# Shifting SBUF tiles to multiples of 256 bytes in a two-block transformer kernel

## The chip, the cores and the metric

The kernel runs on one core of one Trainium2 chip. The metric is the device time of one execution in microseconds (us), the median of several. Nothing is shared with another core.

## The reference: what is computed

Two blocks of two layers each, batch 1, in float32, width 1024. The first block works on 512 latent and 256 context tokens, the second on the 512 latent tokens alone.

```python
# first block, per layer: modulated norm, mixer, residual, squared-relu MLP (hidden width 4096)
x = x + mod_l[:, :, 2] * y_l
x = x + mod_l[:, :, 5] * sq_relu_mlp(modulate(x, norm2_g[layer], mod_l, 3), mlp_w1[layer], mlp_w2[layer])
# layer 0 mixes by an mLSTM and window attention, layer 1 by attention over context and latents
# second block, per layer (hidden width 2816)
def swiglu_half(x, w1, w3, w2):
    return 0.5 * ((jax.nn.silu(x @ w1) * (x @ w3)) @ w2)
x = layer_norm(ALPHA * x + swiglu_half(x, ffn1...), ...)
mix = concatenate([spatial_gating(...), gated_deltanet(...), gla(...)]) @ w_out[l]
x = layer_norm(ALPHA * x + mix, ...)
x = layer_norm(ALPHA * x + swiglu_half(x, ffn2...), ...)
```

## The kernel before

Almost all of the work is dense products of 128x128 blocks. To keep float32 accuracy each factor is split into a high part H and a low part L, both of the type float32r, and `mm3` (L154) issues three matmuls into the same PSUM bank: high by high, high by low, low by high. In a matmul one operand stands in the array (a weight load, 128 columns, ahead of each matmul) and the other moves through it (mostly 512 columns). In the trace a row such as `ps<-hH,wh` names the moving operand first and the standing one second.

Weights arrive by DMA in `wf` (two buffers of 8 KB per partition), ScalarE copies them to `wh`, VectorE takes the difference to `wl` (four buffers of 4 KB each). These three pools are opened first on the right side of SBUF (L205), where addresses are handed out downward from the upper end. All other right-side pools (the residual tiles `xl`, `tm`, the attention keys `kv0`, the tiles of the second block's mixers) lie below them.

On the left side, handed out upward, lie in this order: `const` (identity, masks, `mod`), then `hT`, the transposed activations of the latents, `hH` and `hL` (L216, 128 x 8 x 512 each); then, in the first block, the small tiles `sm1`, then `hTc`, the transposed context activations `hcH` and `hcL` (L326), then the tiles of the stage at hand: the inner features `hid` of the squared-relu MLP (L1156), the rows, keys, values and probabilities of layer 1 (`rows1`, `rows1b`). In the second block there are `sm2` and then, in each gated feed-forward, the pool `hidf` with scratch `sl` (three buffers), the inner features `hidH` and `hidL` (13 buffers each) and behind it the pool `wx` with four more weight buffers.

The dense products have four shapes:

- feature-major (`genA`, and the first products of the MLPs and feed-forwards): a 128-column block of `wh` or `wl` stands, `hH` or `hL` moves with 512 columns (`hcH`, `hcL` with 256).
- second product of the squared-relu MLP (`genP` with `lhs` from `hid`): a block of `hid` stands, `wh` or `wl` moves.
- token-major products of the mixers and of the attention layer (`genP`, `genB`): a block of `hH`, `hL` or `hcH`, `hcL` stands, `wh` or `wl` moves.
- second product of the gated feed-forward (`gen2`): a block of `hidH` or `hidL` stands, `wh` or `wl` moves.

The gate of the gated feed-forward is `glu` (L1833 and on): ScalarE writes Silu of the first product to `sl`, VectorE multiplies it with the second product and 0.5, then ScalarE copies it to `hidH` and VectorE writes the rest to `hidL`. The order of all instructions is fixed when the program is built; a rough clock of the builder weaves the chains of the mixers between the dense products, but no tile's address enters into it.

Of the kernel before, what the change touches and what calls it, by code (L numbers as in the profile page):

```python
# [25 lines left out]
# order of emission in the mixers: priorities of chains, backlog they may see, order of the projections  # L26
# [8 lines left out]
N6, NQ, N5, N5B = 9, 4, 13, 15  # L35

# [11 lines left out]
class Lane:  # L48
    """an engine whose calls are passed on and added to a rough clock, for the order of emission"""
# [53 lines left out]
class Slots:  # L103
    """tiles handed out and given back in the order of emission"""
# [11 lines left out]
class Net:  # L116
# [73 lines left out]
    def right(self, es, name, bufs=1):  # L190
        return es.enter_context(self.tc.tile_pool(name=name, bufs=bufs, side="right", reuse_waits="tile"))

    def pool(self, es, name, **kw):
        return es.enter_context(self.tc.tile_pool(name=name, bufs=1, side="left", reuse_waits="tile", **kw))

# [1 line left out]
    def run(self):  # L197
        with ExitStack() as es:
            self.es = es
            tc, nc, I = self.tc, self.nc, self.I  # L200
            self.flip = False
            cp = self.pool(es, "const")
            self.cp = cp
            self.psp = es.enter_context(tc.tile_pool(name="psum", bufs=8, space=PSUM))
            self.wf, self.wh, self.wl = self.right(es, "wf", 2), self.right(es, "wh", 4), self.right(es, "wl", 4)  # L205
            self.dp = es.enter_context(tc.tile_pool(name="scratch", bufs=1, space=bass.MemoryType.DRAM))
            cm = cp.tile([128, 8, 128], F32, name="cmat")
            nc.sync.dma_start(cm, I["cmat"])
            self.ident, self.U, self.Ub, self.maskF, self.maskB, self.U64, self.S64 = [cm[:, i, :] for i in range(7)]
            self.I64 = cm[:, 7, 0:64]  # L210
            self.ones = cp.tile([128, 128], F32, name="ones")
            nc.vector.memset(self.ones, 1.0)
            self.mhalf = cp.tile([128, 16], F32, name="mhalf")
            nc.vector.memset(self.mhalf, -0.5)
            hp = self.pool(es, "hT")
            self.hT = hp.tile([128, 8, 512], F32R, name="hH"), hp.tile([128, 8, 512], F32R, name="hL")  # L216
            if self.start == "all":
                self.first_specs()
            if self.stop not in ("L0mix", "L0", "L1"):
                self.second_specs()  # L220
            if self.start == "all":
                self.first_block()
            if self.stop not in ("L0mix", "L0", "L1"):
                self.second_block()
            else:
                self.xes.close()
# [10 lines left out]
    # ================= first block =================  # L237
# [3 lines left out]
    def tok(self, t):  # L241
        """features by tokens of tile t: context 0, 1, latents 2..5"""
        a, i = (self.hTc, t) if t < 2 else (self.hT, t - 2)
        c = slice(i * 128, i * 128 + 128)
        return a[0][:, :, c], a[1][:, :, c]
# [12 lines left out]
    def mild(self, i):  # L258
        """pieces whose low parts GpSimd takes: all of them, or the second half of each"""
        n = len(self.specs)  # L260
        if i in SLOW0:
            self.slow |= {n, n + 1}
        if -i - 1 in SLOW0:
            self.slow |= {-n, -n - 1}
# [45 lines left out]
    # feature blocks of layer 0's projection: columns, width, pieces of modulation weights between  # L310
# [34 lines left out]
    def ada_setup(self):  # L345
        nc, I, cp = self.nc, self.I, self.cp
        self.mark("ada")
        cc = self.sm.tile([16, 128], F32, tag="cc", name="cc", bufs=1)
        nc.sync.dma_start(cc[0:8, :], I["c"][0].rearrange("(k p) -> k p", p=128))
        nc.sync.dma_start(cc[8:16, :], I["c_ctx"].rearrange("(k p) -> k p", p=128))  # L350
        gr = self.sm.tile([32, 128], F32, tag="gr", name="gr", bufs=1)
        for i, n in enumerate(("norm1_g", "norm2_g")):
            nc.sync.dma_start(gr[16 * i:16 * i + 16, :], I[n].rearrange("l (k p) -> (l k) p", p=128))
        self.act(cc, cc, AF.Silu)
        p = self.pb.get()
        nc.tensor.transpose(p[:, 0:16], cc, self.ident[0:16, 0:16])
        nc.tensor.transpose(p[:, 16:48], gr, self.ident[0:32, 0:32])
        self.sT = self.sm.tile([128, 8, 32], F32, tag="sT", name="sT", bufs=1)
        nc.vector.memset(self.sT, 0.0)
        nc.vector.tensor_copy(self.sT[:, :, 0:1], p[:, 0:8].unsqueeze(2))  # L360
        nc.vector.tensor_copy(self.sT[:, :, 1:2], p[:, 8:16].unsqueeze(2))
        self.gF = self.sm.tile([128, 2, 2, 8], F32, tag="gF", name="gF", bufs=1)
        nc.vector.tensor_copy(self.gF.rearrange("p a b c -> p (a b c)"), p[:, 16:48])
        self.pb.put(p)
        # [layer, latents or context, part of the modulation, feature block]
        self.mod = cp.tile([128, 2, 2, 6, 8], F32, name="mod")
        self.mD = [[self.dp.tile([128, 512], F32, name=f"mD{l}{s}") for s in range(3)] for l in range(2)]
# [18 lines left out]
    def ada_first(self, c, n, f):  # L386
        """half c of shift and scale of the first norm, two row blocks"""
        r = 64 * c
        if n == 0:
            self.abanks[c] = self.pb.get()  # L390
        for k in range(2):
            for s in range(2):
                self.nc.tensor.matmul(self.abanks[c][r + 32 * s:r + 32 * s + 32, :], lhsT=self.sT[:, 2 * n + k, :], rhs=f[:, k, s, :],
                                      start=n + k == 0, stop=n == 3 and k == 1)
                self.pe(0.43)
        if n == 3:
            self.spawn(self.ch_first(c), 0)
# [44 lines left out]
    def gate_row(self, pool, l, i, r):  # L442
        """row of modulation i (2 or 5) for all partitions"""
# [7 lines left out]
    def ch_mod(self, t, x, l, i, name, tm, keep=True):  # L451
        """modulated rms norm of token tile t, by features and split; x as two halves of 512"""
# [44 lines left out]
    def genP(self, tiles, width, evac, raw=(), lhs=None, gate=None):  # L497
        """token-major product with eight row blocks of weights, token tiles by pairs"""
# [32 lines left out]
    def layer0(self):  # L531
# [9 lines left out]
        # keys of a head above themselves, and their low parts  # L541
# [11 lines left out]
        # norm of the inputs while the modulation is on its way  # L553
# [88 lines left out]
        # -- window attention  # L642
# [171 lines left out]
        def ch_switch():  # L814
            """room for the rest once the window attention is done"""
# [6 lines left out]
        # -- mLSTM  # L822
# [313 lines left out]
    def gated(self, x, p, g):  # L1136
        """x += g * p"""
# [97 lines left out]
    def layer1(self):  # L1235
# [121 lines left out]
        def ch_rl(g, t, rl):  # L1357
            """rows of the reciprocal sums, for all partitions"""
# [157 lines left out]
    def specraw(self, q):  # L1516
        """pieces of the modulation weights, used as they are"""
# [12 lines left out]
    def issue(self):  # L1530
        """loads for which a buffer is free"""
# [12 lines left out]
    def wsplit(self):  # L1544
        """closures that split the next piece"""
# [45 lines left out]
    def ahead(self):  # L1591
        """queue the split of the next weights"""
# [20 lines left out]
    def specA(self, w, c0, n, extra=False):  # L1613
        """columns c0..c0+n of w, output features by 128"""
# [9 lines left out]
    def genA(self, n, evac, more=(), take=tuple):  # L1624
        """n pieces of up to two output tiles of 128 features, 512 tokens; evac gives the bank back"""
# [12 lines left out]
    def genB(self, toks, width, evac):  # L1638
        """token-major, token tiles by pairs; evac gives the bank back"""
# [19 lines left out]
    # ================= second block =================  # L1659
# [81 lines left out]
    def g_layer_norm(self, y, n, eps, g, b):  # L1741
        """in place (y - mean) * rsqrt(var + eps) * g + b over n columns"""
# [15 lines left out]
    def chain_T(self, t, x):  # L1758
        """x transposed and split into the columns of tile t of hT"""
# [37 lines left out]
    def gen2(self, hs, epi):  # L1797
        """token-major product of the hidden tiles with 1024 columns"""
# [24 lines left out]
    def ffn(self, l, p, ln, dump):  # L1823
# [3 lines left out]
        with ExitStack() as es:  # L1827
# [5 lines left out]
            def glu(p1, p3, hs):  # L1833
                s_ = hid.tile([128, 512], F32, tag="sl", name="sl", bufs=3)
# [63 lines left out]
    def mixers(self, l):  # L1898
# [13 lines left out]
        # conv weights by feature, spatial biases by token  # L1912
# [54 lines left out]
        # small constants of the layer  # L1967
# [22 lines left out]
        def ch_gdn_gates():  # L1990
# [31 lines left out]
            # row of the cumulated gates of the chunk for its tokens  # L2022
# [118 lines left out]
        def ch_inv():  # L2141
# [20 lines left out]
            # E for the queries: keys up to the query of the same chunk  # L2162
# [19 lines left out]
        def head_out(out, ov, gate, nh, sq_, p, ev):  # L2182
            """rms norm per head of 64 of ov (PSUM), times gate"""
# [154 lines left out]
        def ch_prep():  # L2338
            """inverses and off-diagonal blocks of a tile as diagonal blocks"""
# [354 lines left out]
```

## Time and profile before

| | |
|---|---|
| median of 3 runs | 3851.73 us (3850.28 to 3855.07) |
| span of the profiled execution | 3851.4 us |
| TensorE matmuls busy | 3754.8 us, 97% of the span |
| weight loads busy | 3016.6 us, 78% |
| VectorE, ScalarE, GpSimd busy | 1893.6, 1316.6, 324.7 us |
| DMA | 379.65 MB, mean 99 GB/s |
| mean granted TensorE clock | 0.990 of full speed |

The profiled execution's span is 0.3 us below the median of the runs. In the chain of work that ended last TensorE holds 86%, VectorE 7%, ScalarE 2%, DMA 1%.

The matmuls of one TensorE queue overlap: the profile shows each from its start to its modelled end, and the next one starts before that. The pace of a stretch is read from the starts: the first and the last row of a timeline, divided by the number of matmuls between.

### The profile page before, as it was taken

Reading aid. Unit: us, or ns where it says so; the run is one execution under the profiler, and the core shown is the slowest. Engines: PE = TensorE matmul, PEld = TensorE weight load, DVE = VectorE, ACT = ScalarE, POOL = GpSimd, SP = SyncE. Lnnn points to the kernel's source line nnn. Section 1 sums busy time; section 2 is a strip of 40 time slices with the busy share of each in tenths; the row PEclk is TensorE's granted clock in tenths of the full one; section 3 lists DMA queues with packets and bytes.
Section 4 is the critical chain, followed back from the end, with each engine's and each line's share of the span. In section 5 each row is a group of like instructions: output and inputs, shape, how many; then the busy total and the mean of one; then the engine's idle time right before and its main releaser. Section 6 shows DMA issues by size and latency. Waiting matters only on the chain.

```text
span 3851.4 us, 46517 instructions
## 1 busy us (share of the span) xinstructions
PE 3754.8 (97%) x18941; PEld 3016.6 (78%) x18941; DVE 1893.6 (49%) x3367; ACT 1316.6 (34%) x2213; POOL 324.7 (8%) x283
## 2 busy tenths in 40 slices
PE   8999899999999999999999999999999999999998
PEld 5676777777877778878888878888888888778887
DVE  4646663333368654443334586433433355864334
ACT  4547441211345532232222543222222225423221
POOL 1202200000011000000000241000000002410000
PEclk9999999999999999999999999999999999999999
DMA  6214542433221122223323421232333234212222
GB/s 241 69 50 143 170 167 99 156 99 102 66 72 57 42 91 88 91 96 99 104 83 121 103 80 66 89 103 82 99 99 104 89 116 102 77 66 93 99 88 82
DMA packets 282310, 379.65 MB, mean 99 GB/s; under 512 B 49224, under 2 KB 207296, under 8 KB 276976
## 3 DMA queue, kind: packets, MB, share of 16 engines
q1 hardware_dynamic: 282096, 376.68, 30.4%
q8 instruction: 148, 2.42, 0.3%
q14 instruction: 66, 0.54, 0.0%
HBM read 359.50 MB, written 17.15 MB: 98 GB/s over the span
## 4 chain that ended last, share of the span: by engine, by line
PE 86%; DVE 7%; ACT 2%; POOL 1%; DMA 1%; issue 1%; SPq 0%; POOLq 0%; ACTq 0%; DVEq 0%
PE ps L142 82%; PE ps L151 3%; POOL r L81 1%; PE ps L380 1%; DVE wl L81 1%; DVE x L81 1%; DVE ui L81 1%; DVE ua L81 1%; DVE hL L81 1%; DVE mx L81 0%; DMA fa<-in_ada_w_dram 0%; DVE st L81 0%; ACT wh L81 0%; DVE tm L81 0%; DVE u L81 0%
## 5 line engine op out<-in xcount | busy, mean ns | idle before, releaser
L81 ACT ACTIVATE wh<-wf 128x1024 fp32r<-128x1024 f32 (+2 forms) x516 | 538.0, 1050 | 1493.7 <-PE ps L142 1261.4
L81 DVE TENSOR_TENSOR wl<-wf,wh 128x1024 fp32r<-128x1024 f32 (+2 forms) x496 | 600.3, 1216 | 809.2 <-ACT wh L81 808.8
L142 PE MATMUL ps<-hH,wh 128*128 128x512 f32 (+1 forms) x2336 | 885.6, 380 | 6.8 <-ACT hH L81 5.6
L142 PE MATMUL ps<-hL,wh 128*128 128x512 f32 (+1 forms) x2336 | 881.8, 378 | 0.0
L142 PE MATMUL ps<-hH,wl 128*128 128x512 f32 (+1 forms) x2336 | 881.0, 377 | 0.0
L142 PEld LDWEIGHTS ps<-hH,wh 128*128 128x128 f32 x2336 | 440.0, 189 | 108.0 <-issue 9.5
L142 PEld LDWEIGHTS ps<-hL,wh 128*128 128x128 f32 x2336 | 440.8, 189 | 88.8 <-DVE ss L81 1.7
L142 PEld LDWEIGHTS ps<-hH,wl 128*128 128x128 f32 x2336 | 440.7, 189 | 88.3
L142 PE MATMUL ps<-wh,hid 128*128 128x512 f32 x1280 | 405.1, 395 | 0.0
L81 POOL TENSOR_TENSOR r<-rs,mhalf 128x1 f32<-128x1 f32 (+4 forms) x112 | 135.9, 1215 | 2775.4 <-DVE rs L81 2760.7
L142 PE MATMUL ps<-wh,hH 128*128 128x512 f32 (+3 forms) x800 | 315.3, 395 | 3.8 <-ACT uc L81 2.1
L142 PE MATMUL ps<-wh,hL 128*128 128x512 f32 (+3 forms) x800 | 303.4, 380 | 4.5 <-DVE hL L81 4.2
L142 PE MATMUL ps<-wl,hH 128*128 128x512 f32 (+3 forms) x800 | 302.3, 379 | 1.0 <-DVE wl L81 1.0
L142 PEld LDWEIGHTS ps<-wh,hid 128*128 128x128 f32 x1280 | 239.6, 187 | 58.0
L142 PE MATMUL ps<-wh,hidH 128*128 128x512 f32 x704 | 274.3, 390 | 0.0
L142 PE MATMUL ps<-wl,hidH 128*128 128x512 f32 x704 | 274.0, 389 | 0.0
L142 PE MATMUL ps<-wh,hidL 128*128 128x512 f32 x704 | 273.9, 389 | 0.0
L142 PE MATMUL ps<-wl,hid 128*128 128x512 f32 x640 | 252.5, 394 | 0.0
L81 DVE SCALAR_TENSOR_TENSOR sl<-sl,ps 128x512 f32<-128x512 f32 x88 | 60.5, 687 | 259.7 <-PE ps L142 259.6
L142 PEld LDWEIGHTS ps<-wh,hH 128*128 128x128 f32 x800 | 152.1, 190 | 43.3 <-issue 5.8
L142 PEld LDWEIGHTS ps<-wh,hL 128*128 128x128 f32 x800 | 152.3, 190 | 36.9 <-DVE hL L81 7.4
L142 PEld LDWEIGHTS ps<-wl,hH 128*128 128x128 f32 x800 | 152.7, 191 | 26.2 <-DVE wl L81 1.5
(369 smaller groups left out, 4740.7 us busy)
## 6 DMA issues: line engine op xcount, KB each, us to landing
wf<-in_ffn_w_dram SPq DMA_DIRECT2D x120, 1024.0 KB
wf<-in_mlp_w_dram SPq DMA_DIRECT2D x64, 1024.0 KB
wf<-in_ada_w_dram SPq DMA_DIRECT2D x40, 1024.0 KB
wf<-in_w_in_dram SPq DMA_DIRECT2D x24, 1024.0 KB
wf<-in_ffn_w_dram SPq DMA_DIRECT2D x24, 512.0 KB
wf<-in_ab_w_in_dram SPq DMA_DIRECT2D x10, 1024.0 KB
fa<-in_ada_w_dram SPq DMA_DIRECT2D x16, 512.0 KB
wf<-in_w_out_dram SPq DMA_DIRECT2D x16, 512.0 KB
```

The costliest lines, as they stand in the source:

```text
L81: r = f(*a, **kw)
L142: self.nc.tensor.matmul(out, lhsT=l, rhs=r, start=start, stop=stop)
L151: self.nc.tensor.transpose(out, in_, self.ident)
L380: self.nc.tensor.matmul(self.abank[32 * j:32 * j + 32, :], lhsT=self.sT[:, k, :], rhs=f[:, 512 * j:512 * j + 512], start=k == 0, stop=k == 7)
```

## The change

Every pool whose name is in a new table gets one more tile, allocated first and never used, so that all later tiles of that side move by its size. A pool `edge` is opened ahead of the weight buffers on the right side. The scratch `sl` of the gated feed-forward has two buffers in place of three. Nothing else changes but comments, which are taken out: the instructions, their order and their operands' sizes are the same.

```diff
+PAD = {'const': 64, 'sm1': 160, 'hidf': 224, 'edge': 224}
...
     def right(self, es, name, bufs=1):
-        return es.enter_context(self.tc.tile_pool(name=name, bufs=bufs, side="right", reuse_waits="tile"))
+        p = es.enter_context(self.tc.tile_pool(name=name, bufs=bufs, side="right", reuse_waits="tile"))
+        if name in PAD:
+            p.tile([128, PAD[name] // 4], F32, name="pad" + name, bufs=1)
+        return p
 
     def pool(self, es, name, **kw):
-        return es.enter_context(self.tc.tile_pool(name=name, bufs=1, side="left", reuse_waits="tile", **kw))
+        p = es.enter_context(self.tc.tile_pool(name=name, bufs=1, side="left", reuse_waits="tile", **kw))
+        if name in PAD:
+            p.tile([128, PAD[name] // 4], F32, name="pad" + name)
+        return p
...
+            self.right(es, "edge")
             self.wf, self.wh, self.wl = self.right(es, "wf", 2), self.right(es, "wh", 4), self.right(es, "wl", 4)
...
-                s_ = hid.tile([128, 512], F32, tag="sl", name="sl", bufs=3)
+                s_ = hid.tile([128, 512], F32, tag="sl", name="sl", bufs=2)
```

## Rows read from the trace of the kernel before

**Rows 1.** Page, head and section 1: span, and busy time of each engine.

```profile
span 3851.4 us, 46517 instructions
PE 3754.8 (97%) x18941; PEld 3016.6 (78%) x18941; DVE 1893.6 (49%) x3367; ACT 1316.6 (34%) x2213; POOL 324.7 (8%) x283
```

**Rows 2.** Busy time by stretch: length, engines, granted clock, DMA share, GB/s.

```profile
60.00:541.00 481.00, 453.06 (x2305) 338.09 (x2303) 284.20 (x784) 249.92 (x601) 97.05 (x80) 0.98 0.38 126
541.00:1106.00 565.00, 565.00 (x2902) 453.21 (x2903) 229.21 (x352) 145.86 (x228) 3.75 (x7) 1.00 0.30 100
1106.00:1358.00 252.00, 238.12 (x1156) 190.39 (x1154) 189.32 (x489) 128.66 (x291) 25.54 (x30) 0.98 0.18 57
1734.00:2110.00 376.00, 375.67 (x1754) 311.08 (x1753) 137.32 (x158) 97.32 (x120) 6.05 (x4) 1.00 0.31 99
2110.00:2418.00 308.00, 298.84 (x1919) 242.08 (x1919) 215.54 (x400) 132.25 (x204) 81.02 (x63) 0.98 0.29 85
```

**Rows 3.** Groups by form, TensorE: moving, standing operand, shape, count, busy, mean ns.

```profile
L142 PE MATMUL ps<-hH,wh 128*128 128x512 f32 x1952 | 776.7, 398 | 0.0
L142 PE MATMUL ps<-wh,hid 128*128 128x512 f32 x1280 | 405.1, 395 | 0.0
L142 PE MATMUL ps<-wh,hidH 128*128 128x512 f32 x704 | 274.3, 390 | 0.0
L142 PE MATMUL ps<-wl,hH 128*128 128x512 f32 x640 | 256.1, 401 | 0.0
L142 PE MATMUL ps<-wl,hcH 128*128 128x512 f32 x128 | 52.5, 410 | 0.0
L142 PE MATMUL ps<-hH,wl 128*128 128x256 f32 x384 | 108.5, 284 | 0.0
L142 PE MATMUL ps<-hcH,wl 128*128 128x256 f32 x256 | 71.3, 278 | 0.0
```

**Rows 4.** Timeline of TensorE, feed-forward, feature-major: start, length; 104 rows.

```profile
1925.84 0.40 PE L142 MATMUL ps<-hL,wh 128*128 128x512 f32 x1
...
1949.87 0.40 PE L142 MATMUL ps<-hH,wl 128*128 128x512 f32 x1
```

**Rows 5.** Timeline, squared-relu MLP, second product: 105 matmuls.

```profile
629.62 0.63 PE L142 MATMUL ps<-wh,hid 128*128 128x512 f32 x2
...
653.89 0.39 PE L142 MATMUL ps<-wl,hid 128*128 128x512 f32 x1
```

**Rows 6.** Timeline, output projection of a mixer, token-major: 69 matmuls.

```profile
2395.95 0.39 PE L142 MATMUL ps<-wh,hH 128*128 128x512 f32 x1
...
2411.81 0.40 PE L142 MATMUL ps<-wh,hL 128*128 128x512 f32 x1
```

**Rows 7.** Timeline, gated feed-forward, second product: 107 matmuls.

```profile
1867.79 0.39 PE L142 MATMUL ps<-wl,hidH 128*128 128x512 f32 x1
...
1891.82 0.39 PE L142 MATMUL ps<-wh,hidL 128*128 128x512 f32 x1
```

**Rows 8.** Timeline, context half of the MLP: two groups of 24.

```profile
565.80 0.28 PE L142 MATMUL ps<-hcH,wh 128*128 128x256 f32 x1
...
568.63 0.39 PE L142 MATMUL ps<-hH,wh 128*128 128x512 f32 x1
...
573.52 0.28 PE L142 MATMUL ps<-hcH,wh 128*128 128x256 f32 x1
...
576.24 0.40 PE L142 MATMUL ps<-hH,wh 128*128 128x512 f32 x1
```

**Rows 9.** Timeline of VectorE and ScalarE around the gate: scratch freed, next Silu.

```profile
1936.21 0.69 DVE L81 TENSOR_TENSOR hidL<-sl,hidH 128x512 fp32r<-128x512 f32 x1
...
1946.18 0.58 ACT L81 ACTIVATE sl<-ps 128x512 f32<-128x512 f32 x1
```

**Rows 10.** Timeline of TensorE just after a context group: three slow steps.

```profile
1004.99 0.40 PE L142 MATMUL ps<-hH,wh 128*128 128x512 f32 x1
...
1005.71 0.39 PE L142 MATMUL ps<-hH,wh 128*128 128x512 f32 x1
```

## The prediction, made before the change was run

> **What bounds the kernel now.** I read the page's head first: matmuls keep TensorE busy for 97% of the span, and no other engine passes half [rows 1]. Busy time by stretch then tells where TensorE waits at all. In the squared-relu MLP (541 to 1106 us) and in a gated feed-forward (1734 to 2110) it is busy from end to end; only around the mixers and the attention does it stand still, 28 us of 481, 14 of 252 and 9 of 308 [rows 2] (the second mixer, 3168 to 3472, repeats the last). So outside these stretches nothing but the pace of the matmuls sets the time, and in them it sets most.
>
> The groups by form give the counts, not the pace, because neighbours overlap and a mean of 390 or 398 ns counts time twice. Each group stands there for more: `mm3` makes three of each token-major or feature-major product, and high and low parts are equally many. That makes 5856 feature-major matmuls of 512 columns (3 x 1952), 1920 of the squared-relu MLP's second product (1280 with `wh` moving and half as many with `wl`), 1920 token-major with `hH`/`hL` standing, 384 with `hcH`/`hcL` standing, and 2112 of the gated feed-forward's second product (3 x 704). Of 256 columns there are 1152 with `hH`/`hL` moving and 768 with `hcH`/`hcL` [rows 3].
>
> The pace comes from starts in the timelines, in stretches where TensorE waits for nobody and the granted clock is full:
>
> - feature-major: 24.03 us over 103 steps, 233.3 ns each [rows 4]
> - MLP, second product: 24.27 us over 104 steps, 233.4 ns [rows 5]
> - token-major: 15.86 us over 68 steps, 233.2 ns [rows 6]
> - gated feed-forward, second product: 24.03 us over 106 steps, 226.7 ns [rows 7]
>
> The fourth differs from the second in one thing that I find: which tile stands. [...] The mixed case is as telling: context groups of 24 matmuls of 256 columns, same tiles, run once at 2.83 us (117.9 ns each) and once at 2.72 us (113.3 ns) [rows 8]. A loss that locks into one of two steady values while weight loads and moving data are both being read looks like two streams of reads getting into each other's way, with a phase that decides how often.
>
> **What the change does to addresses.** The pads tell the old positions. Every tile between is a multiple of 256 bytes long, so 64 bytes in `const` that bring `hT` to a multiple mean that it stood at remainder 192; 64 + 160 = 224 bytes for all that lies behind `sm1` in the first block mean 32 for `hcH`, `hcL` and `hid`; 64 + 224 = 288 = 256 + 32 for `hidf` mean 224 for `hidH` and `hidL`; and 224 off the upper end mean 224 for `wf`, `wh`, `wl`. Remainders of moving and standing operand are then: feature-major 192 and 224; MLP second product 224 and 32; token-major 224 and 192 (or 32); gated second product 224 and 224. The one product whose two operands have the same remainder is the one that runs at 226.7. After the change all four have 0 and 0. The layer-1 keys, values and probabilities go from 32 to 0 too; the mixers' tiles on the right only move by 32 bytes.
>
> **The sum.** Forecast: the same remainder for both operands gives the pace of rows 7 everywhere. That is 233.3 - 226.7 = 6.6 ns per 512-column matmul that is not there yet.
>
> - Feed-forwards and MLPs: the token-major products (1920 + 384 = 2304) all stand in the mixers and the attention, and some 580 feature-major ones do as well (six weight pieces of 48 matmuls in each of two mixers, by the code). Of 5856 + 1920 + 2304 = 10,080 this leaves 7,200 in stretches without waits: 7,200 x 6.6 = 47.5 us, all on the path.
> - Mixers and attention: 2,880 x 6.6 = 19 us. There chains of VectorE and ScalarE run beside the products and end some of the waits of rows 2; they do not get faster, and a shorter product covers less of them. Bounds 0 and 19; I take two thirds, 13 us, because TensorE waits only for 60 of 1345 us.
> - 256 columns: same rule, 117.9 to 113.3, 4.6 ns for 1152 + 768 = 1920: 8.8 us (some groups are at 113.3 already, while the halves with `hH` are a little slower than 118). 9 us.
> - `gen2`: stays at 226.7, 0 us. Other engines: ScalarE and VectorE are below half and off the path, DMA at a third of its time; whether their instructions gain by the addresses costs or gives nothing outside the waits already counted.
> - `sl` in two buffers: Silu number n now waits until the low part of number n-2 is taken. In the steady part that ends at 1936.21 + 0.69 = 1936.90, and the Silu comes at 1946.18, 9.3 us later [rows 9]; 3% off the pace takes some 0.3 us of that. A new wait would hold ScalarE, and with it the copies of weights queued behind it, for which TensorE waits: up to a gap in each of 22 column blocks per feed-forward. Only where two gates follow one another at once, in the first block, is the margin smaller. 0 us.
> - Pads themselves: no instruction, 0 us.
>
> Sum: 47.5 + 13 + 9 = 69.5 us. 3851.4 - 69.5 = 3781.9; the runs' median is 0.3 us above that span, so 3782.
>
> [...]
>
> **Rivals.**
>
> 1. Nothing changes: 3852. Rows 7 would owe their pace to something else in the gated second product, such as that its consecutive triples go to alternating PSUM banks while the others stay in one bank for 12 or 24 matmuls. Against it: inside the triple, where the bank stays, the steps are as short as between triples. For it: I have only one product with equal remainders in long steady runs. 13%.
> 2. [...] 17% together, from 3740 down. [...]
> 3. Only some products gain, say the MLP's and the token-major ones with weights moving, where both operands shift, while the feature-major ones stay: (1920 + two thirds of 2304) x 6.6 + 5 us for the context groups = 28 us, 3824. 12%.
> 4. Slower: equal remainders of exactly 0 put the two reads on each other at each load, and the steady value that results is worse than before. The nearest rows are three steps of 0.72 / 3 = 240 ns just after a context group, where the phase is wrong for a moment [rows 10]. If that became the steady pace: 10,080 x 6.7 + 2112 x 13.3 + 2112 x 4 = 68 + 28 + 8 = 104 us, 3956. It decides from the point where a feature-major step exceeds 233.3 ns, and it would show in the gated second product most, which has its good pace to lose. 13%.
>
> **How the numbers follow.** The forecast has 45%, for 3760 to 3800: its unknowns are the 0 to 19 us of the mixers (3788 to 3769) and a few us of the attention's operands. With rival 2 (17%) and 3 (12%) faster by over 0.2% has 74%. A measurement of this kernel can tell about 0.2% (8 us) from no change; within that lies rival 1 with 13%, and slower is rival 4 with 13%. The range leaves out rival 4 and the lower half of rival 2: 3690 to 3858 holds the forecast, rivals 1 and 3 and the 220 ns case, some 80%.
>
> **What would show it.** In the timelines at the places of rows 4 to 6, steps of 226.7 ns and not 233.3 prove the forecast; in rows 7's place the step should stay. All context groups should be at 2.72 us. Busy time by stretch should shrink by 3% in the feed-forwards' first products and in the MLPs, by 2% or less around the mixers, with TensorE's waits there somewhat longer. If the steps shrink only where both operands moved (MLP second product), relative position isn't the reason. [...] A gap before Silu or a wait of TensorE for `wh` in the feed-forwards would show that two `sl` buffers are too few. The prediction is wrong if the step has nothing to do with addresses.

## The result, and the profile after

The median is 3804.4 us (3800.1 to 3806.6) against 3851.2 us of the kernel before on the same chip: a ratio of 0.9875, 95% interval 0.9861 to 0.9889. The change makes the kernel faster by 46.8 us. The profiled execution of the kernel after has a span of 3801.5 us, 49.9 us less than that of before.

The head of the page of after (line numbers are four to eleven higher than before; `mm` is now L146). It answers to [rows 1]:

```profile
span 3801.5 us, 46499 instructions
PE 3701.4 (97%) x18941; PEld 3018.5 (79%) x18941; DVE 1891.8 (50%) x3367; ACT 1317.2 (35%) x2213; POOL 326.4 (9%) x283
```

Same matmuls, same weight loads; TensorE is busy for 53.4 us less and still for 97% of the span. (The 18 instructions that the page has less than before are none of these engines' work.) The other engines keep their busy time to within 2 us. So the matmuls follow one another faster; nothing was moved aside.

Busy time by stretch, kernel after, over the work of [rows 2] (first mixer, squared-relu MLP, attention of layer 1, a gated feed-forward, a mixer):

```profile
59.20:539.60 480.40, 452.00 (x2303) 339.25 (x2302) 281.67 (x783) 249.82 (x601) 98.37 (x87) 0.97 0.38 126
539.60:1094.40 554.80, 554.76 (x2902) 455.32 (x2903) 229.19 (x352) 145.87 (x228) 3.77 (x7) 1.00 0.31 102
1094.40:1345.20 250.80, 234.58 (x1156) 188.59 (x1155) 190.12 (x490) 129.65 (x292) 25.43 (x30) 0.99 0.19 58
1710.40:2081.30 370.90, 370.54 (x1752) 312.18 (x1752) 137.08 (x157) 97.21 (x120) 6.05 (x4) 1.00 0.31 100
2081.30:2387.90 306.60, 296.76 (x1920) 242.33 (x1919) 216.29 (x399) 132.26 (x204) 81.90 (x63) 0.98 0.30 85
```

Measured between the same matmuls in both traces, the two MLPs are 10.3 us shorter each and the four gated feed-forwards 5.1, 6.2, 6.2 and 6.1 us: 44.2 us in all. First mixer, attention and the two other mixers give 0.5, 1.8, 1.5 and 1.2 us: 5.0 us. The gain lies where TensorE hardly ever waits. Of the small amounts, those of the first mixer and the attention can't be told from the difference between two executions: in the run without the shift of the weight buffers, below, which has none of the faster paces, the two stretches came out 4.6 and 2.2 us shorter than in before.

The pace, as starts in the timeline of TensorE in after, at full clock and without a wait. First the feature-major product, the MLP's second product and the gated second product, as [rows 4, 5, 7] show them for before (105, 105 and 106 steps):

```profile
1899.94 0.39 PE L146 MATMUL ps<-hH,wl 128*128 128x512 f32 x1
...
1923.74 0.39 PE L146 MATMUL ps<-hH,wl 128*128 128x512 f32 x1
```

```profile
628.79 0.39 PE L146 MATMUL ps<-wl,hid 128*128 128x512 f32 x1
...
652.59 0.39 PE L146 MATMUL ps<-wl,hid 128*128 128x512 f32 x1
```

```profile
1841.92 0.39 PE L146 MATMUL ps<-wl,hidH 128*128 128x512 f32 x1
...
1865.72 0.39 PE L146 MATMUL ps<-wl,hidH 128*128 128x512 f32 x1
```

All three take 23.80 us for 105 steps, 226.7 ns each. Before it was 233.3, 233.4 and 226.7. The two products that changed have come to the pace of the one that didn't.

The context groups of 24 matmuls of 256 columns, the same two places as [rows 8]:

```profile
563.07 0.28 PE L146 MATMUL ps<-hcH,wh 128*128 128x256 f32 x1
...
565.95 0.40 PE L146 MATMUL ps<-hH,wh 128*128 128x512 f32 x1
...
570.73 0.28 PE L146 MATMUL ps<-hcH,wh 128*128 128x256 f32 x1
...
573.60 0.40 PE L146 MATMUL ps<-hH,wh 128*128 128x512 f32 x1
```

The groups take 565.95 - 563.07 = 2.88 and 573.60 - 570.73 = 2.87 us, 119.6 to 120 ns each, and all 31 full groups of the kernel settle at 120.0. Before, 24 of them settled at 117.8 and seven at 113.3. Here the change costs time.

Two rows answer to [rows 9], VectorE's freeing of the scratch and the Silu that takes it:

```profile
1910.54 0.68 DVE L85 TENSOR_TENSOR hidL<-sl,hidH 128x512 fp32r<-128x512 f32 x1
...
1920.20 0.58 ACT L85 ACTIVATE sl<-ps 128x512 f32<-128x512 f32 x1
```

The buffer is free at 1911.22, the Silu comes 9.0 us later. Over all 88 gates the least distance is 6.2 us, at the first blocks. Two buffers are enough.

### The profile page after: what moved, and what is told of

It reads as the page before. It is cut to its first block, busy times and chain, and to the rows that moved or that the text cites. A ratio compares the mean times of both kernels' runs of the same rounds, so it can differ in the third digit from the quotient of the medians.

```text
span 3801.5 us, 46499 instructions
## 1 busy us (share of the span) xinstructions
PE 3701.4 (97%) x18941; PEld 3018.5 (79%) x18941; DVE 1891.8 (50%) x3367; ACT 1317.2 (35%) x2213; POOL 326.4 (9%) x283
## 4 chain that ended last, share of the span: by engine, by line
PE 85%; DVE 8%; ACT 2%; DMA 2%; POOL 2%; issue 1%; SPq 0%; POOLq 0%; DVEq 0%; ACTq 0%
PE ps L146 81%; PE ps L155 3%; POOL r L85 1%; DVE ui L85 1%; DVE wl L85 1%; PE ps L391 1%; DVE x L85 1%; DVE ua L85 1%; DVE hL L85 1%; DVE mx L85 0%; DMA fa<-in_ada_w_dram 0%; ACT wh L85 0%; DVE st L85 0%; DVE tm L85 0%; DVE u L85 0%
## 5 line engine op out<-in xcount | busy, mean ns | idle before, releaser
L146 PE MATMUL ps<-hH,wh 128*128 128x512 f32 (+1 forms) x2336 | 873.7, 375 | 6.9 <-ACT hH L85 5.6
L146 PE MATMUL ps<-hL,wh 128*128 128x512 f32 (+1 forms) x2336 | 870.2, 373 | 0.3 <-DVE hL L85 0.3
L146 PE MATMUL ps<-hH,wl 128*128 128x512 f32 (+1 forms) x2336 | 869.7, 373 | 0.0
L146 PEld LDWEIGHTS ps<-hH,wh 128*128 128x128 f32 x2336 | 440.3, 189 | 96.3 <-issue 9.5
L146 PEld LDWEIGHTS ps<-hL,wh 128*128 128x128 f32 x2336 | 441.6, 189 | 76.7 <-DVE hL L85 1.9
L146 PEld LDWEIGHTS ps<-hH,wl 128*128 128x128 f32 x2336 | 441.3, 189 | 76.5
L146 PE MATMUL ps<-wh,hid 128*128 128x512 f32 x1280 | 397.6, 390 | 0.0
L146 PE MATMUL ps<-wh,hH 128*128 128x512 f32 (+3 forms) x800 | 313.0, 392 | 4.1 <-ACT uc L85 2.1
L146 PE MATMUL ps<-wh,hL 128*128 128x512 f32 (+3 forms) x800 | 302.2, 378 | 4.2 <-DVE hL L85 3.9
L146 PE MATMUL ps<-wl,hH 128*128 128x512 f32 (+3 forms) x800 | 300.0, 376 | 1.1 <-DVE wl L85 1.1
L146 PEld LDWEIGHTS ps<-wh,hid 128*128 128x128 f32 x1280 | 240.1, 188 | 49.6
L146 PE MATMUL ps<-wh,hidH 128*128 128x512 f32 x704 | 274.2, 390 | 0.0
L146 PE MATMUL ps<-wh,hidL 128*128 128x512 f32 x704 | 273.9, 389 | 0.0
L146 PE MATMUL ps<-wl,hidH 128*128 128x512 f32 x704 | 273.9, 389 | 0.0
L146 PE MATMUL ps<-wl,hid 128*128 128x512 f32 x640 | 249.1, 389 | 0.0
L146 PEld LDWEIGHTS ps<-wh,hH 128*128 128x128 f32 x800 | 152.5, 191 | 42.1 <-issue 5.8
L146 PEld LDWEIGHTS ps<-wh,hL 128*128 128x128 f32 x800 | 152.2, 190 | 34.5 <-DVE hL L85 7.2
L146 PEld LDWEIGHTS ps<-wl,hH 128*128 128x128 f32 x800 | 152.6, 191 | 24.6 <-DVE wl L85 1.6
```

The costliest lines, as they stand in the source:

```text
L146: self.nc.tensor.matmul(out, lhsT=l, rhs=r, start=start, stop=stop)
```

## Experiments

In the first four expectations theory A is the forecast's: only whether moving and standing operand have the same remainder counts. From here on "difference" is the remainder of moving less standing operand, mod 256 bytes.

**A map of pairs.** A synthetic kernel with none of the reference's work: eight moving and eight standing tiles at remainders 0, 32, ... 224 (`ma` to `mh`, `sa` to `sh`), every pair as a group of 24 matmuls, 512 and 256 columns, forth and back.

```python
for order in (pairs, pairs[::-1]):
    for cols in (512, 256):
        for m, s in order:
            for k in range(24):
                nc.tensor.matmul(b[:, 0:cols], lhsT=st[s][:, (k % 4) * 128:(k % 4) * 128 + 128], rhs=mv[m][:, 0:cols], ...)
```

> Not the model: only matmuls. 24 at a time of the same shape, float32r, the moving and the standing tile at each of the 8 x 8 pairs of remainders 0, 32, ... 224 modulo 256 (tiles ma to mh move, sa to sh stand), first all pairs with 512 columns, then with 256, then the same again in the opposite order. All else of the computation is left out. Theory A (equal remainders let the two reads run in step): the 8 pairs with equal remainders take 226.7 ns per 512-column step, the other 56 take 233.3; with 256 columns 113.3 against 117 to 120. Theory B (position itself counts, a multiple of 256 is good): row or column 0 is better than the others, and pairs such as (32, 32) or (160, 160) are at 233.3. Theory C (it has nothing to do with addresses, the gated second product owed its pace to alternating PSUM banks): all 64 pairs alike at 233.3.

Timeline of TensorE in the map: each row is a group of 24, so that the distance of two starts is 24 steps. 512 columns, moving remainder 64 (`mc`), standing 32, 64, 96:

```profile
103.05 5.76 PE L41 MATMUL b<-mc,sb 128*128 128x512 f32 x24
108.64 5.61 PE L41 MATMUL b<-mc,sc 128*128 128x512 f32 x24
114.09 5.75 PE L41 MATMUL b<-mc,sd 128*128 128x512 f32 x24
119.68 2.50 PE L41 MATMUL b<-mc,se 128*128 128x512 f32 x10
```

5.59, 5.45 and 5.59 us. Taken over the last 15 steps of each group, all eight equal pairs are at 226.7 ns, whatever their remainder. The 56 unequal ones lie between 228.9 and 234.5, nearly all at 232 to 234.5 and only those of difference 64 at 229 (one of these at 233.3 on the second pass). (One equal pair, the first in the run, began its first pass with 12 steps of 427 ns, the pace that the kernel has at a granted clock of 0.50, and was at 226.7 on the second.) PSUM banks alternate alike for all pairs. So the pace belongs to the pair of positions.

256 columns, moving remainder 32 (`mb`), standing 96, 64, 32, 0 in the second pass:

```profile
1050.69 2.90 PE L41 MATMUL b<-mb,sd 128*128 128x256 f32 x24
1053.43 3.00 PE L41 MATMUL b<-mb,sc 128*128 128x256 f32 x24
1056.27 3.04 PE L41 MATMUL b<-mb,sb 128*128 128x256 f32 x24
1059.15 2.97 PE L41 MATMUL b<-mb,sa 128*128 128x256 f32 x24
```

The equal pair (`mb,sb`) is the slowest with 2.88 us, 120.0 ns; the one of difference 192 (`mb,sd`) takes 2.74 us and is at 113.3 ns once settled. All equal pairs are at 120; of the eight pairs with difference 192, two are at 113.3 and six at 117.8 in the first pass, seven at 113.3 and one at 117.7 in the second. Only difference 96, at 119.7 to 120.3, is as slow as equality throughout. What is best for 512 columns is among the worst for 256.

**Without the shift of the weight buffers.** The weights stay at 224, all else goes to 0.

```diff
-PAD = {'const': 64, 'sm1': 160, 'hidf': 224, 'edge': 224}
+PAD = {'const': 64, 'sm1': 160, 'hidf': 224}
```

> The change without the pad of the right side: activations and inner tiles at remainder 0, weight buffers back at 224. Now no product has equal remainders, not even the gated second one that had them before. Theory A: all four products at 233.3 ns per step, so the time before and 2112 x 6.6 = 14 us more: 3865 us. Theory B (the activations' position is what counts): feature-major products keep 226.7, their 5856 x 6.6 = 38 us stay: some 3815 us.

3859.9 us, ratio 1.0023 (1.0014 to 1.0033): slower than before. Timeline of TensorE, feature-major and gated second product:

```profile
1915.84 0.39 PE L146 MATMUL ps<-hH,wh 128*128 128x512 f32 x1
...
1939.64 0.39 PE L146 MATMUL ps<-hH,wh 128*128 128x512 f32 x1
```

```profile
1854.92 0.40 PE L146 MATMUL ps<-wh,hidL 128*128 128x512 f32 x1
...
1878.72 0.40 PE L146 MATMUL ps<-wh,hidL 128*128 128x512 f32 x1
```

102 steps in 23.80 us, 233.3 ns, in both. The gated second product has lost the pace that it had in before: its sum of steps goes from 479.2 to 491.2 us, and the feature-major ones stay where they were. These are the paces of theory A; the 12 us of the gated product stand for the 14 that it had added up. Three of the four pads without the fourth are worth nothing.

**All at 160.** Equality kept, the multiple of 256 given up.

```diff
-PAD = {'const': 64, 'sm1': 160, 'hidf': 224, 'edge': 224}
+PAD = {'const': 224, 'sm1': 160, 'hidf': 224, 'edge': 64}
```

> All dense operands at remainder 160, none at a multiple of 64, 128 or 256. Theory A: as after the change, 226.7 ns in all four products, 3804 us. Theory B: 233.3 ns, 3851 us, or 3865 if the gated second product loses its pace too.

3808.5 us, ratio 0.9894 (0.9877 to 0.991), the interval overlaps that of after. Feature-major timeline:

```profile
1904.85 0.39 PE L146 MATMUL ps<-hL,wh 128*128 128x512 f32 x1
...
1928.65 0.39 PE L146 MATMUL ps<-hL,wh 128*128 128x512 f32 x1
```

105 steps in 23.80 us: 226.7 ns, without any operand at a multiple of 256. Sums of steps against before: feature-major -35.5 us, MLP's second product -12.1, context groups +2.2; in after -36.5, -12.1 and +2.2.

**Multiples of 64 that differ.** Weights at 0, `hT` at 128, hidden tiles and context at 64.

```diff
-PAD = {'const': 64, 'sm1': 160, 'hidf': 224, 'edge': 224}
+PAD = {'const': 192, 'sm1': 96, 'hidf': 160, 'edge': 224}
```

> Weights at 0, transposed latents at 128, both kinds of inner tiles and the context at 64: the feature-major pair differs by 128, the two second products by 64, each position a multiple of 64. Theory A with a period of 256: 233.3 ns everywhere, 3865 us. With a period of 128: feature-major at 226.7, the rest at 233.3, about 3865 - 38 = 3827. With a period of 64, or theory B in the form that multiples of 64 are enough: all at 226.7, 3804.

3858.5 us, ratio 1.0021 (1.0011 to 1.003). Gated second product:

```profile
1860.05 0.39 PE L146 MATMUL ps<-wh,hidL 128*128 128x512 f32 x1
...
1883.85 0.39 PE L146 MATMUL ps<-wh,hidL 128*128 128x512 f32 x1
```

102 steps in 23.80 us, 233.3 ns, at a difference of 192. The feature-major product, whose operands differ by 128, decides on a period of 128:

```profile
1922.09 0.39 PE L146 MATMUL ps<-hH,wl 128*128 128x512 f32 x1
...
1945.79 0.39 PE L146 MATMUL ps<-hH,wl 128*128 128x512 f32 x1
```

102 steps in 23.70 us, 232.4 ns: a little better than before, far from 226.7. Positions at multiples of 64 or 128 aren't enough: among the positions of this run and the map, only equality mod 256 gives 226.7.

**Three buffers for `sl`.** The other part of the change undone alone.

```diff
-                s_ = hid.tile([128, 512], F32, tag="sl", name="sl", bufs=2)
+                s_ = hid.tile([128, 512], F32, tag="sl", name="sl", bufs=3)
```

> The kernel after with the scratch sl of the gate in three buffers again; all positions as after. Theory (two buffers cost nothing, because a freed buffer lies about 9 us ahead of the Silu that wants it): the time of after, 3804 us, within 0.2% (3797 to 3812), and every pace as after. Rival (two buffers hold ScalarE, and the feed-forwards gave back part of their gain that way): each of the four gated feed-forwards is shorter than after's 371, 364, 374 and 363 us, by up to the 6.5 us in all by which the time missed the forecast's part for them.

3804.9 us, ratio 0.9871 (0.9856 to 0.9885). The first gated feed-forward, busy time by stretch:

```profile
1706.50:2077.90 371.40, 371.01 (x1754) 312.69 (x1753) 137.41 (x158) 97.26 (x120) 6.06 (x4) 1.00 0.31 100
```

371.4 us against 370.9 in after, the other three equal within 0.1 us. The two-buffer scratch costs nothing and brings nothing in time.

**All at 192, and the mixers' extra weights too.** In after a pool `wx`, opened behind `sm2` for the mixers' last product, stands at 32.

```diff
-PAD = {'const': 64, 'sm1': 160, 'hidf': 224, 'edge': 224}
+PAD = {'sm1': 160, 'sm2': 224, 'edge': 32}
```

> All operands at remainder 192, context and the mixers' extra weights wx too; otherwise as after. Theory: as after everywhere, context products of 256 columns at 120 ns, and only the last product of each mixer improves, from alternating 227 and 231 to 236 ns to a steady 227: some 100 matmuls of two mixers by 6 ns, -1 us. 3801 to 3806 us. Rival (position itself counts as well, 0 is better or worse than 192): the feature-major pace differs from 226.7 ns.

3803.6 us, ratio 0.9871 (0.9855 to 0.9888). Paces as in after (feature-major sum -36.4 us against before), and the output projection of a mixer at the place of [rows 6], where `wx` takes half of the weights, comes to the good pace:

```profile
2365.84 0.40 PE L146 MATMUL ps<-wh,hH 128*128 128x512 f32 x1
...
2381.26 0.39 PE L146 MATMUL ps<-wh,hL 128*128 128x512 f32 x1
```

68 steps in 15.42 us, 226.8 ns, where after has 231.8 (below). Over both mixers of the second block the token-major products sum to 194.9 us against 195.6, a gain of 0.7 us, about the 1 us that was expected; a median can't show it. The sum over the whole kernel can't either: the token-major gain with `hT` is 7.8 us here and 5.8 in after, but 2.8 and 4.4 in the two runs below that put `wx` on the same remainder too, because the waits of the first mixer differ from execution to execution.

**Context at difference 192.** As the run before, but `hcH`, `hcL` at 128.

```diff
-PAD = {'const': 64, 'sm1': 160, 'hidf': 224, 'edge': 224}
+PAD = {'sm1': 96, 'hid': 64, 'sm2': 224, 'edge': 32}
```

> All operands of the 512-column products at remainder 192 in place of 0, the mixers' extra weights wx among them (they stand at 32 after the change, beside hT at 0), but the context hcH, hcL at 128, so that moving less standing is 192 mod 256 for the 256-column context products: the difference that gave 113.3 ns in the map, in place of 120 ns for equal remainders. Theory (only differences mod 256 count, and each width has its own best one): 512-column paces as after; context products of 256 columns from 119.7 ns to between 113.3 and 117.8, that is -1.5 to -5 us over 768; token-major products with hcH standing (384) back from 229 to 233, +1 to +2 us; the last product of each mixer, where wx takes every second half, no longer breaks its lock, about -1 us in all. Sum 3798 to 3804 us. Rival (the short products' pace is a matter of chance, not of the difference): they stay at 119 to 120 ns, and the time is 3804 to 3806.

3800.4 us, ratio 0.9865 (0.985 to 0.988): inside the expected times, but not to be told from after. The MLP of layer 0 takes 553.2 us in place of 554.8, the context matmuls sum to 91.8 us in place of 94.6. Two neighbouring context groups in its timeline:

```profile
577.58 0.28 PE L146 MATMUL ps<-hcH,wh 128*128 128x256 f32 x1
...
580.41 0.39 PE L146 MATMUL ps<-hH,wh 128*128 128x512 f32 x1
...
588.09 0.28 PE L146 MATMUL ps<-hcH,wh 128*128 128x256 f32 x1
...
589.45 0.28 PE L146 MATMUL ps<-hcH,wh 128*128 128x256 f32 x1
```

The first runs at 2.83 us / 24 = 117.9 ns, the last 12 steps shown of the second at 1.36 us / 12 = 113.3. So it goes on: the groups alternate between 117.8 and 113.3 to 113.6 to the end of the MLP. The map's two values for that difference are found again, one half each. So the difference helps the context products, as the theory had it, but the value that a group falls into is not set by the positions alone.

**Fine steps, and interruptions.** Synthetic: one standing tile at 0, the moving slice shifted by as little as 4 bytes; then groups of 6 to 48 matmuls of 512 columns, each behind four float32 matmuls of 128 columns (L52, eight rows in the trace).

> Synthetic, none of the reference's work: groups of 24 matmuls of float32r, one standing tile at remainder 0, the moving slice 0 to 252 bytes behind remainder 0 in steps down to 4 bytes, for 512, 384 and 256 columns, forth and back; then groups of 6, 12, 24 and 48 matmuls of 512 columns, at difference 0 and at 32 bytes, with four float32 matmuls of 128 columns ahead of each. Theory: what counts is a line of 32 bytes or more, so at 4 to 28 bytes the pace is between those of 0 and 32 or equal to one of them; 512 columns 226.7 ns at 0 and 233 at 32 to 224; 256 columns 120 ns at 0. After an interruption both start alike at 231 to 234 ns, and the equal pair falls to 226.7 after 6 to 12 matmuls while the other stays: a group of 6 gains nothing, one of 12 less than half, one of 48 most. Rival (no locking: the equal pair is at 226.7 from its first matmul): groups of 6 gain as much per matmul as groups of 48, and the products of the mixers missed their gain for another reason.

Equality is sharp at one end and not at the other. 512 columns, last 15 steps of a group, first pass: 226.7 ns at 0, 236.6 at 4 bytes, 233.3 at 8, 231.7 at 16, 226.7 again at 28 and at 252, 233.5 at 32. So four bytes ahead of a multiple of 32 can be as good as equality, and four behind is the worst of this run; "a line of 32 bytes" isn't the rule. Differences of 48 and 64 bytes had two values, 233.2 and 233.3 in the first pass, 230.0 and 228.9 in the second. For 256 columns a difference of 16 bytes gave 113.3 in both passes, 192 too, and 64 gave 113.3 in one and 117.7 in the other. For 384 columns equality took 173.3 ns, but so did 28, 64 and 252 bytes, and in one of the two passes also 4, 8, 160, 192 and 224. The interrupted part, timeline; the first group of 48 is at difference 0, the second at 32 bytes:

```profile
606.65 11.14 PE L40 MATMUL b<-mv,st 128*128 128x512 f32 x48
617.63 1.05 PE L52 MATMUL b<-idn,x 128*128 128x128 f32 x8
618.43 11.44 PE L40 MATMUL b<-mv,st 128*128 128x512 f32 x48
629.72 1.05 PE L52 MATMUL b<-idn,x 128*128 128x128 f32 x8
```

10.98 us against 11.29. Step by step an equal group goes 314, 232, 231, 227, 226, 227, ... or 318, 231, 236, 228, 233, 231, 226, 227, ... ns (the first step holds the end of the float32 matmuls); the unequal one goes round 231, 235, 234 to its end. Means over a group: 6 matmuls 246 to 249 ns against 248 to 251; 12: 235.5 to 237.3 against 241; 48: 229 against 235. The equal pair has to lock in, over two to five steps more, and a group of six gains some 2 ns per step in place of 6.6.

**Context 16 bytes off.** The best short pace of the fine steps, put into the kernel.

```diff
-        self.hTc = hcp.tile([128, 8, 256], F32R, name="hcH"), hcp.tile([128, 8, 256], F32R, name="hcL")
+        hc = hcp.tile([128, 4104], F32R, name="hc")
+        self.hTc = tuple(hc[:, a:a + 2048].rearrange("p (k t) -> p k t", k=8) for a in (4, 2052))
...
-PAD = {'const': 64, 'sm1': 160, 'hidf': 224, 'edge': 224}
+PAD = {'sm1': 160, 'hid': 224, 'sm2': 224, 'edge': 32}
```

> As the run with all operands at 192 and wx too, but the context's hcH and hcL 16 bytes behind that remainder (one tile holds both). The fine map gave 113.3 ns for 256 columns at a difference of 16 bytes, from the first matmuls on. Theory (the map carries over to the kernel): the 768 context matmuls of 256 columns go from about 120 to 113.3 ns, -5 us; the 384 token-major ones with hcH standing, now 16 bytes off the other way, lie somewhere between 226.7 and 236 ns, -1 to +3 us; the rest as in the run that it starts from. 3797 to 3803 us, MLP of layer 0 about 5 us shorter than after's 554.8. Rival (the map's short products lock so only where one pair repeats without a change of tiles): context stays at 118 to 120 ns and the MLP of layer 0 at 555 us.

3804.9 us, ratio 0.9882 (0.9865 to 0.9898), MLP of layer 0 555.0 us: no gain. Of 31 context groups 28 settle at 118.5 to 118.7 ns and 3 at 113.3. The rival had it right: what locks at once where one pair repeats doesn't do so in the kernel, where high and low tiles alternate and 512-column groups lie between. Groups with the same tiles and positions settle at either value, so something besides position selects it; no run varied what a group comes after alone, so what that is stays open.

**Narrower standing tiles.** Synthetic, as the fine steps, with 128, 96, 64 and 32 standing columns. The 213.3 ns below are an estimate: half of the 426.7 ns that 512 columns take in before at a granted clock of 0.50 (6 steps from 479.45 to 482.01 us).

> Synthetic, none of the reference's work: groups of 24 matmuls as in the fine map, but the standing tile 128, 96, 64 or 32 columns wide, moving slice at difference 0, 32, 128 and 224 bytes, 512 and 256 columns, forth and back; then differences of 240, 208, 48 and 16 bytes at full width. Theory (what is lost is reads of the standing tile meeting reads of the moving one): the loss over 213.3 ns shrinks with the width of the standing tile, from 13.3 ns (equal) and 20 ns (unequal) at 128 columns to about a half of that at 64 and a quarter at 32, and equal and unequal draw together. Rival (a loss per matmul that has nothing to do with how much is read for the standing tile): the same 226.7 and 233 ns at every width.

The weight loads themselves get shorter, from a mean of 191 ns at 128 columns to 162, 134 and 108. Steps in ns at 512 columns, last 15 of each group, first pass, by difference:

| standing columns | 0 | 32 | 128 | 224 |
|---|---|---|---|---|
| 128 | 226.7 | 233.3 | 232.3 | 233.2 |
| 96 | 229.9 | 233.3 | 231.4 | 228.9 |
| 64 | 230.0 | 231.0 | 229.3 | 231.6 |
| 32 | 231.7 | 232.7 | 230.3 | 239.9 |

Neither theory nor rival. The loss over 213.3 ns does not shrink with the number of standing columns: at 32 columns it is 17 to 27 ns in this pass. But it isn't a constant either; equality has its good pace at 128 columns alone. On the second pass difference 32 had 226.7 at 96 and 226.6 at 32 standing columns, so that the same pair has two steady values here as well. The number of standing columns alone doesn't set the loss. At 256 columns equality is slow with 128 standing columns only (119.7 and 120.0 ns in the two passes): it takes 116.0 with 96 and 113.3 with 64. The four further differences at full width gave 236.8 (240 bytes), 234.7 (208), 233.5 (48) and 231.5 ns (16) for 512 columns.

## Why the prediction was right, and where it was off

The forecast is the one that came true: same remainders give the pace of [rows 7], and it holds to the tenth of a nanosecond. Direction, place and mechanism as far as addresses go were right. There was luck in it: that equality is what counts was read off a single product, and other differences (28 and 252 bytes) turned out as good. The reason that the prediction gave, two streams of reads in each other's way, was a guess from paces and is not shown by any run. The median, 3804.4, lies 22 us above the 3782 predicted, and just above the 3760 to 3800 of the likeliest case. By the terms of the sum, from start-to-start steps of each group in both traces:

| term | forecast, us | measured, us |
|---|---|---|
| feature-major (5856) and MLP's second product (1920), with the share of the mixers | -50.1 | -36.5 - 12.1 = -48.6 |
| token-major with `hT`, `hc` standing (2304) | -10.1 | -6.5 |
| 256 columns moving `hH` (1152), `hc` (768) | -8.8 | +1.0 + 2.2 = +3.2 |
| gated second product | 0 | -0.2 |
| all else | 0 | about +2 |

(The first two lines divide the prediction's 47.5 and 13: of the 2,880 matmuls in mixers and attention 2304 are token-major and some 580 feature-major, at two thirds of 6.6 ns. The measured column is one execution of each kernel. In the three-buffer run, whose positions are the same, the lines are -47.7, -8.4, +5.0, -0.2 and -2.5, so all but the first and the fourth are known to some 2 to 5 us.)

1. **The large term** was right within 3%: 48.6 us over 7776 matmuls is 6.25 ns each, and where nothing interrupts 6.6.

2. **256 columns: the wrong sign.** The step that failed is "same rule, 117.9 to 113.3". It read [rows 8] as if the good value belonged to equal positions, though the rows said nothing of the kind: their operands were at 32 and 224, a pair without equality, and still had the good value at times. Their difference is 64, for which the fine steps have the same two values, 113.3 and 117.7. The map gives equality 120.0, among the worst for this width. These 12 us (14 by the three-buffer run) are the largest part of the miss. They are also one reason why the MLPs shrank by 1.8% (10.3 of 565 us) and not by the 3% of the prediction's signs. The point "all context groups should be at 2.72 us" was the prediction's own test, and it came out at 2.87.

3. **Mixers and attention: too much.** The prediction took two thirds of the full gain on the ground that TensorE waits little there. It left out that a product that is cut up by transposes and other small matmuls never runs long at its steady pace: the token-major steps without a wait (those below 300 ns) went from 233.3 ns on average to 229.8, about half of the 6.6 ns. Waits took a part as well, as the prediction said they would: in the stretches of [rows 2] TensorE stood still for 252.00 - 238.12 = 13.9 us of the attention and 9.2 of a mixer, in the same rows of after for 16.2 and 9.8. A token-major run of after, behind a transpose:

```profile
478.96 0.60 PE L155 MATMUL ps<-cmat,v 128*128 128x128 f32 x4
...
479.63 0.40 PE L146 MATMUL ps<-wl,hH 128*128 128x512 f32 x1
...
481.94 0.39 PE L146 MATMUL ps<-wh,hL 128*128 128x512 f32 x1
...
489.42 0.39 PE L146 MATMUL ps<-wh,hL 128*128 128x512 f32 x1
```

   2.31 us for the first 10 steps, 231 ns; 7.48 us for the 33 steps from 481.94 on, 226.7. The interrupted groups of the synthetic run show the same by themselves.

4. **The output projection at [rows 6]'s place** missed a point of the prediction, which wanted 226.7 there. In after it begins and ends so:

```profile
2365.83 0.40 PE L146 MATMUL ps<-wh,hH 128*128 128x512 f32 x1
...
2381.59 0.40 PE L146 MATMUL ps<-wh,hL 128*128 128x512 f32 x1
```

   68 steps in 15.76 us, 231.8 ns. By the addresses half of its weights are those of `wx` at 32, beside `hT` at 0, and equal and unequal stretches take turns. "After the change all four have 0 and 0" overlooked this pool; with it on the same remainder the place runs at 226.8, as the run at 192 shows. In all it is a matter of under 1 us.

5. **The clock made no net difference.** Its mean over the profiled execution is 0.990 of full speed in before and 0.991 in after. But it shifts time about in the first mixer. In after TensorE works there for 1.18 of the 4.00 us from 316 on, and the next 4.00 us have a granted clock of 0.52; in before it works for 1.54 of the same 4.00 us, and the next 4.00 are at 1.00. The first mixer took 477.5 us with three `sl` buffers (mean clock 0.98), 480.4 in after (0.97) and 486.2 with the context at 128 (0.96), with the token-major steps of all three within 1 ns of one another. So a term of a few microseconds in the first mixer can't be read from one execution. The lower level, a granted clock of 0.50, shows something else. Token-major product of before, an unequal pair (224 and 192), busy time and timeline:

```profile
479.50:482.70 3.20, 3.20 (x9) 2.52 (x8) 0.69 (x1) 0.04 (x1) 0.00 (x0) 0.50 1.05 413
```

```profile
479.45 0.63 PE L142 MATMUL ps<-wh,hH 128*128 128x512 f32 x1
...
482.01 0.63 PE L142 MATMUL ps<-wh,hH 128*128 128x512 f32 x1
```

   At a granted clock of 0.50 the 6 steps take 2.56 us, 426.7 ns each. Half of that, 213.3 ns, is an estimate for 512 columns at full clock, where the same pair takes 233.2 [rows 6], 20 ns more. In after, with equal positions, nearly all token-major steps at this level are at 426 to 427 ns as well, such as 3 steps in 1.28 us from 177.32 to 178.60. So in these rows the positions make a difference at the upper level alone.

6. **`sl` and the pads** cost nothing, as the sum had it: the three-buffer run shows it, and the margin is 6.2 us where it is least.

**The rivals.** No change at all (PSUM banks as the cause of [rows 7]'s pace) falls with the map, where banks alternate for all pairs and the pace doesn't. Faster than the forecast, from 3740 down, and the 220 ns case of the range: no run shows such a pace; some 226.7 ns is the lowest steady one of 512 columns in any run, at any of the positions tried. Only moving weights gain: falls with the feature-major 226.7. Slower at exactly 0: falls for 512 columns; 256 columns did get slower, but by equality and not by the 0, since the context groups lose the same 2.2 us with all at 160. (In that rival's sum the last term took 2112 for the 1920 short matmuls, which is under 1 us.)

The position of the standing operand counts. In the map 24 steps with the same moving tile at 64 take 5.45 us beside a standing tile at 64 and 5.59 beside one at 32 or 96, which settle at 226.7 and 233.3 ns. What passes between the two streams, if anything does, is not shown by any run; the narrow tiles only show that the loss doesn't shrink with the number of standing columns.

**Open.** The mechanism behind the numbers; why difference 192 has two steady values at 256 columns, and what selects them in the kernel; why 28 and 252 bytes are as good as 0; why the positions make no difference at a granted clock of 0.50. No trace here shows reads by themselves.

## What to carry to other kernels

Where TensorE is busy from end to end, take its pace from starts in the timeline, compare products of one shape with one another, and write their operands' positions beside it; two paces at one clock were worth 1.25% here for a few hundred bytes of padding. For float32r products of 512 columns with a weight load each, put moving and standing tiles on the same remainder mod 256 bytes, whichever it is, and all of them: one pool left behind undoes the gain of every product that it takes part in, as the weights left at 224 did. Don't carry the rule to another width, to fewer standing columns or to products cut into short groups without measuring: at 256 columns equality was the wrong choice.

## What the runs showed of the hardware

- 512 columns, float32r, 128 standing columns, full clock: 226.7 ns at equal remainders mod 256, 228.9 to 234.5 at the other differences by 32 bytes, 236.6 at 4 bytes. No steady pace of 512 columns came below 226.6; half of the 426.7 ns at a granted clock of 0.50 is 213.3, an estimate.
- At a granted clock of 0.50 the same products take 426.7 ns at unequal positions (before) as at equal ones (after). At full clock 226.7 and 233.3 ns at 512 columns lie 6.6 ns apart, 113.3 and 120.0 at 256 columns 6.7; other steady paces, such as 228.9 and 117.8, lie between.
- 256 columns: 120.0 ns at equality, 113.3 at best (differences 16, 64 and 192, none of them in every run), and two steady values for the same pair.
- The good pace isn't there from the start: some three to six steps after an interruption, most of them between 228 and 236 ns, then 226.7.
- Narrower standing tiles aren't faster with 512 columns moving at equality: 231.7 ns for 32 standing columns at difference 0 against 226.7 for 128, although the weight load takes 108 ns in place of 191.
